# Where matmul operands lie in SBUF: weights of the seven-product tiles and of the down projection shifted by 128 bytes in a decoder layer on one core

## The chip, the core and the metric

One core of a Trainium2 chip runs one program: TensorE (matmuls; its weight loads are listed on their own as PEld), VectorE (DVE), ScalarE (ACT), GpSimd (POOL) and SyncE, which issues the weight transfers from HBM. The metric is device time in microseconds (us) of one execution.

## The reference

One decoder layer on x of 512 tokens by 1024 columns, all in float32:

```python
x = x + 0.5 * swiglu(rms_norm(x, g_ffn1), w_ffn1_gate, w_ffn1_up, w_ffn1_down)
h = rms_norm(x, g_mix); proj = h @ w_in
# sliding-window attention with sinks, causal depthwise convolution with layer norm,
# and cross-attention into 256 memory tokens, from column groups of proj
x = x + concatenate([y_attn, y_conv, y_mem]) @ w_out
x = x + 0.5 * swiglu(rms_norm(x, g_ffn2), w_ffn2_gate, w_ffn2_up, w_ffn2_down)

def swiglu(x, w_gate, w_up, w_down):
    return (silu(x @ w_gate) * (x @ w_up)) @ w_down
```

The feed-forward width is 2816: 22 tiles of 128 columns, called f = 0 to 21 below.

## The kernel before

Activations are held transposed, with 128 columns of the model on the partitions and 512 tokens along the free axis. To keep float32 accuracy, every large operand is split in two float32r parts, hi (a rounded copy) and lo (what the rounding lost), and each product is three matmuls: weights hi by moving hi, weights hi by moving lo, weights lo by moving hi. In a projection with 512 moving columns (helper `mm3`) these are L330, L331 and L332; in the products of a feed-forward tile (`product`) they are L434, L435 and L436, with 256 moving columns.

Each feed-forward stage (`ffn`, called as "fast1" and "fast2") runs f = 0 to 3 directly, with full gate and up projections (L330 to L332, moving tiles `xh`, `xl`). The other 18 tiles use a seven-product scheme of the Strassen kind over the 2 by 2 blocks gate/up by token halves: seven products of four blocks each, that is 84 matmuls of 256 columns (moving tiles `bh`, `bl`). The down projections (L330 to L332, moving tiles `hh`, `hl`, 512 columns) are done in rounds between the tiles, most of them after the fifth of the seven products. Between the two stages `mixing` does attention, convolution and memory attention by a list of steps in a fixed order (`ORDER`).

Weights pass through the class `Weights`. SyncE loads them into one of four `wraw` buffers (L138), ACT writes the hi part (L158, `whi`) and DVE the lo part (L159, `wlo`), each into a rotation of four buffers of 1024 columns. The second half of one weight tile of each seven-product tile goes to a buffer pair of its own, `vhi` and `vlo`, from the stage's pool (`extra`).

All these buffers lie in SBUF at fixed addresses. What counts below is the address within a partition, modulo 256 bytes. All `whi`, `wlo`, `vhi` and `vlo` start at 0; blocks of weights within them are 512 bytes apart, so that every weight block starts at 0. `xh`, `xl`, `yh`, `yl`, `hh`, `hl` start at 64. `bh` and `bl` start at 192 in the first feed-forward stage and at 64 in the second: the argument `shift` of `ffn`, 128 in the first call and 0 in the second, puts a pad of that many bytes ahead of the stage's pool, and a second pad after `bh` and `bl` brings both to one total. So the start of the moving tile less that of the weights is 192 in the first stage's products, 64 in the second's, and 64 in all down projections and other projections.

Two small things in `mixing` matter as well. `consts` (L745) fills a constant tile `avg` on POOL and a mask tile `maskb` of two rows of 512 columns on DVE, early in the stage. `ln_mean` (L1036) sums the two convolution tiles, takes their mean by a matmul with `avg` (L1042), and DVE subtracts it (L1044); squares on ACT (L1050), a sum on DVE (L1052) and small matmuls (L1057) follow.

Of the kernel before, what the change touches and what calls it, by code (L numbers as in the profile page):

```python
# [25 lines left out]
F32 = mybir.dt.float32  # L29
F32R = mybir.dt.float32r  # L30
BF16 = mybir.dt.bfloat16
# [5 lines left out]
P = 128  # L37
T = 512
# [43 lines left out]
class Weights:  # L82
# [5 lines left out]
    def __init__(self, nc, pool, dma_ahead, conv_ahead, bufs):  # L88
        self.nc, self.pool = nc, pool
        self.dma_ahead, self.conv_ahead, self.bufs = dma_ahead, conv_ahead, bufs  # L90
        self.loads, self.items = [], []
        self.raw, self.after, self.split, self.piece = {}, {}, {}, {}
        self.sums = {}
        self.extra = None
        self.by_hand = 2
        self.loaded = self.done = self.at = 0

    def add(self, ap):

        self.loads.append(ap)  # L100
        i = len(self.loads) - 1
        self.items.append((i, int(np.prod(ap.shape[1:])), "w", lambda: self.raw[i]))

    def add_pair(self, gate, up, mid):

        self.loads += [gate, up]
        i = len(self.loads) - 2
        self.after[i + 1] = lambda: self.make_sums(i)
        self.items.append((i, 1024, "w", lambda: self.raw[i]))
        self.items.append((i + 1, 1024, "w", lambda: self.sums[i][0]))  # L110
        self.items.append((i + 1, 1024, "w", lambda: self.sums[i][1]))
        for ap in mid:
            self.add(ap)
        self.items.append((i + 1, 512, "v", lambda: self.raw[i + 1][:, 512:]))

    def make_sums(self, i):
        nc = self.nc
# [23 lines left out]
    def split_to(self, n):  # L141
        nc = self.nc
        while self.done < min(n, len(self.items)):
            i = self.done
            need, cols, tag, src = self.items[i]
            self.load_to(need + 1)
            if need in self.after:
                self.after.pop(need)()
            pool = self.pool if tag == "w" else self.extra
            width = 1024 if tag == "w" else 512  # L150
            bufs = self.bufs[1:] if tag == "w" else (1, 1)
            hi = pool.tile([P, width], F32R, tag=tag + "hi", name=f"{tag}hi{i}", bufs=bufs[0])
            lo = pool.tile([P, width], F32R, tag=tag + "lo", name=f"{tag}lo{i}", bufs=bufs[1])
            if i < self.by_hand:
                self.piece[i] = (src(), hi, lo)
            else:
                raw = src()
                nc.scalar.copy(hi[:, :cols], raw[:, :cols])  # L158
                nc.vector.tensor_tensor(lo[:, :cols], raw[:, :cols], hi[:, :cols].bitcast(F32), op=ALU.subtract)  # L159
            self.split[i] = (hi, lo)  # L160
            self.done += 1
            if i >= self.by_hand:
                self.load_to(need + 1 + self.dma_ahead)
# [33 lines left out]
def layer(tc, ctx, a):  # L197
    nc = tc.nc
# [9 lines left out]
    def nm(s):  # L208
        uid[0] += 1
        return f"{s}_{uid[0]}"  # L210
# [14 lines left out]
        return tmp.tile([P, n], F32, tag=f"s{n}", name=nm("s"), bufs=6)  # L225


    W = Weights(nc, wpool, dma_ahead=3, conv_ahead=3, bufs=(4, 4, 4))

    def flat(w):  # L230
        return w.rearrange("p k m -> p (k m)")
# [1 line left out]
    def ffn_weights(n, memory):  # L233
        gu = a[f"wgu{n}"]

        def down(r, g):
            lo, hi = ROUNDS[r]
            m = per_load(r)
            return a[f"wd{n}"][g * m : (g + 1) * m, :, lo:hi].rearrange("d p k m -> p d (k m)")

        for f in range(NF):
            pre, mid, post = steps(f)
            for d in pre:
                W.add(down(*d))
            if f < N_DIRECT:
                W.add(flat(gu[f, 0]))
                W.add(flat(gu[f, 1]))
            else:
                W.add_pair(flat(gu[f, 0]), flat(gu[f, 1]), [down(*d) for d in mid])
            for d in post:  # L250
                W.add(down(*d))
            if memory and f == MEM_F:
                for t in range(2):
                    W.add(flat(a["wmk"][t]))
                for c in range(2):
                    W.add(flat(a["wmv"][:, 4 * c : 4 * c + 4]))
        r = len(ROUNDS) - 1
        for g in range(KT // per_load(r)):
            W.add(down(r, g))

    ffn_weights(1, True)
    for t in range(12):
# [116 lines left out]
                PE.transpose(ps[:, s], self.bc[:, s], ident)  # L379
            DVE.tensor_copy(rb, ps)  # L380

    def ffn(pool, norm, first, gain, hooks, next_gain, last, shift):
        if shift:
            pool.tile([P, shift // 4], F32, name=nm("shift"))
        h_hi = [None] * NF
        h_lo = [None] * NF
        W.extra = pool
# [19 lines left out]
        def blocks(k):  # L407
# [9 lines left out]
            bh[k] = pool.tile([P, 7, 256], F32R, tag="bh", name=nm("bh"), bufs=4)  # L417
            bl[k] = pool.tile([P, 7, 256], F32R, tag="bl", name=nm("bl"), bufs=4)
            if k == 0:
                pool.tile([P, (192 - shift) // 4], F32, name=nm("shift"))  # L420
            ACT.copy(bh[k][:, 4:7], raw[:, 0:3])
            DVE.tensor_tensor(made[:, B_T3 : B_Q1 + 1], raw[:, 1:3], raw[:, 3:4].to_broadcast([P, 2, 256]), op=ALU.subtract)
            DVE.scalar_tensor_tensor(made[:, B_Q2], made[:, B_T3], -1.0, b11, op0=ALU.mult, op1=ALU.subtract)
# [284 lines left out]
    hooks[MEM_F - 1] = [lambda: piece(2), lambda: piece(3)]  # L708
    hooks[MEM_F], hooks[MEM_F + 1] = [sums, p1], [p2]
    with tc.tile_pool(name="fast1", bufs=1) as pool:  # L710
        norm = ffn(pool, norm, STARTS, C_G1, hooks, C_GM, False, 128)

    with tc.tile_pool(name="mix", bufs=1) as mix:
        norm = mixing(tc, nc, a, mix, W, norm, locals())

    with tc.tile_pool(name="fast2", bufs=1) as pool:
        ffn(pool, norm, [[0, 1, 2, 3, 4, 5, 6], [7]], C_G2, {}, None, True, 0)


def mixing(tc, nc, a, mix, W, norm, e):  # L720
# [14 lines left out]
    vtok = mix.tile([P, NB, P], F32, name="vtok")  # L735
    for i in range(2):
        POOL.memset(pad[:, i, 0:30], 0.0)
    avg = mix.tile([P, P], F32, name="avg")
    maskb = mix.tile([P, 2, T], BF16, name="maskb")
    identb = mix.tile([P, P], BF16, name="identb")  # L740
    nsink = mix.tile([P, 8], F32, name="nsink")
    maskf = work()[:, :256]
    nc.scalar.dma_start(maskf, a["mask"])

    def consts():  # L745
        POOL.memset(avg, 1.0 / 256.0)
        DVE.tensor_copy(maskb[:, :, 0:256], maskf.unsqueeze(1).to_broadcast([P, 2, 256]))
        DVE.tensor_copy(maskb[:, :, 256:512], maskf.unsqueeze(1).to_broadcast([P, 2, 256]))
        DVE.memset(maskb[:, 0, 0:128], -1e30)
        DVE.tensor_copy(identb, ident)  # L750
        DVE.tensor_scalar(nsink, par[:, C_SINK : C_SINK + 8], -1.0, None, op0=ALU.mult)

# [85 lines left out]
    class Attend:  # L838
# [10 lines left out]
        def scores(self, j):  # L849

            self.banks[j] = banks = [sc_bank(), sc_bank()] if j == 0 else [mm_bank(), mm_bank()]
            if self.win:
                for h in range(2):
                    PE.matmul(banks[h], identb, maskb[:, j], start=True, stop=False, skip_group_check=True)
            for i in range(2):
                n = 2 * j + i
                c = self.cols(n)
                for h in range(2):
                    rows = slice(h * HD, (h + 1) * HD)
                    ks = slice((n - 1) * P + c.start, (n - 1) * P + c.stop) if self.win else slice(0, ML)  # L860
                    PE.matmul(  # L861
                        banks[h][:, i * ML + c.start : i * ML + c.stop], self.q[rows, n * P : (n + 1) * P],
                        self.kt[rows, ks], start=not self.win, stop=True, skip_group_check=True,
                    )
# [171 lines left out]

    def ln_mean():
        pump(TAPS)
        both = work()
        DVE.tensor_tensor(both, conv[:, 0], conv[:, 1], op=ALU.add)  # L1040
        mean = tp_bank()
        PE.matmul(mean, avg, both, start=True, stop=True)  # L1042
# [161 lines left out]
```

## Time and profile before

| | us |
|---|---|
| median of 3 runs | 891.36 |
| lowest and highest of them | 890.57, 891.64 |
| the profiled execution | 892.07 |
| its span | 890.1 |
| PE busy in the span | 878.1 |
| DVE busy | 713.4 |
| ACT busy | 440.0 |

The profiled execution is one run with the hardware profiler on; its span goes from the first instruction's start to the last one's end, and 2.0 us of its time lie outside. Matmuls are pipelined, and the length that the profile gives one (280 ns for 256 columns) overlaps the next. Its pace, the time from one matmul's start to the next one's, has to be worked out from the starts in the timeline. Those are given to 10 ns, so a pace is taken over many matmuls: last start less first, divided by the number of steps.

### The profile page before, as it was taken

How to read it: one execution, taken by the hardware profiler on the slowest of the kernel's cores; microseconds unless marked ns; L12 is line 12 of the kernel's file. 1: busy time of each engine (PE TensorE's matmuls, PEld its weight loads, DVE VectorE, ACT ScalarE, POOL GpSimd, SP SyncE). 2: the span in 40 equal slices, each digit the busy share in tenths (PEclk: the TensorE clock that was granted, in tenths of full speed). 3: DMA queues.
4: the chain of work that ended last, by engine and by line, in shares of the span. 5: the costliest groups of instructions: out<-in, count | busy, mean ns of one | idle time of the engine just before them, and what ended most of it. 6: DMA issues, size and time to landing. Idle time of an engine off the chain costs nothing.

```text
span 890.1 us, 13999 instructions
## 1 busy us (share of the span) xinstructions
PE 878.1 (99%) x5525; PEld 771.7 (87%) x5525; DVE 713.4 (80%) x1122; ACT 440.0 (49%) x733; POOL 45.6 (5%) x38
## 2 busy tenths in 40 slices
PE   7999999999999999999999999999999999999998
PEld 3889999999999999888666788889999999999997
DVE  6999978986796886769999766999887868667872
ACT  6354554544563444533928754444554444444540
POOL 6000000000020000300020011000000000000000
PEclk9999999999999999999999999999999999999999
DMA  5522333333333244231010232314333332332312
GB/s 194 166 95 81 109 120 107 113 102 118 111 128 123 92 119 142 72 100 60 9 52 13 83 117 74 103 64 142 95 96 119 96 118 83 109 116 73 119 48 95
DMA packets 34082, 88.45 MB, mean 99 GB/s; under 512 B 3168, under 2 KB 7008, under 8 KB 34016
## 3 DMA queue, kind: packets, MB, share of 16 engines
q1 hardware_dynamic: 32864, 85.99, 30.5%
q10 hardware_dynamic: 1152, 1.57, 0.5%
q8 instruction: 43, 0.70, 0.3%
q14 instruction: 23, 0.19, 0.1%
HBM read 85.45 MB, written 2.10 MB: 98 GB/s over the span
## 4 chain that ended last, share of the span: by engine, by line
PE 94%; DVE 3%; DMA 1%; issue 1%; ACT 0%; SPq 0%; DVEq 0%; ACTq 0%
PE mm L330 15%; PE mm L332 15%; PE mm L331 15%; PE mm L435 11%; PE mm L434 11%; PE mm L436 11%; PE sc L435 2%; PE sc L434 2%; PE sc L436 2%; PE sc L330 1%; PE sc L332 1%; PE sc L331 1%; PE tp L922 1%; PE sc L861 1%; DMA x<-in_xT 1%; DVE conv L786 1%
## 5 line engine op out<-in xcount | busy, mean ns | idle before, releaser
L435 PE MATMUL mm<-bl,whi 128*128 128x256 f32 x864 | 242.3, 280 | 0.0
L434 PE MATMUL mm<-bh,whi 128*128 128x256 f32 x864 | 242.2, 280 | 0.0
L436 PE MATMUL mm<-bh,wlo 128*128 128x256 f32 x864 | 241.9, 280 | 0.0
L158 ACT CAST whi<-wraw 128x1024 fp32r<-128x1024 f32 (+2 forms) x122 | 124.5, 1023 | 130.6 <-PE mm L331 51.0
L159 DVE TENSOR_TENSOR wlo<-wraw,whi 128x1024 fp32r<-128x1024 f32 (+2 forms) x122 | 144.7, 1187 | 35.6 <-ACT whi L158 35.3
L436 PEld LDWEIGHTS mm<-bh,wlo 128*128 128x128 f32 x864 | 163.5, 189 | 0.0
L434 PEld LDWEIGHTS mm<-bh,whi 128*128 128x128 f32 x864 | 162.3, 188 | 1.2 <-ACT kept L449 0.2
L435 PEld LDWEIGHTS mm<-bl,whi 128*128 128x128 f32 x864 | 162.3, 188 | 1.1
L330 PE MATMUL mm<-hh,whi 128*128 128x512 f32 (+1 forms) x356 | 138.5, 392 | 0.0
L332 PE MATMUL mm<-hh,wlo 128*128 128x512 f32 (+1 forms) x356 | 138.2, 390 | 0.0
L331 PE MATMUL mm<-hl,whi 128*128 128x512 f32 (+1 forms) x356 | 137.4, 387 | 0.0
L159 DVE TENSOR_TENSOR wlo<-s,whi 128x1024 fp32r<-128x1024 f32 x72 | 88.3, 1228 | 34.4 <-ACT whi L158 33.7
L158 ACT CAST whi<-s 128x1024 fp32r<-128x1024 f32 x72 | 75.4, 1048 | 56.3 <-PE mm L435 40.2
L332 PEld LDWEIGHTS mm<-hh,wlo 128*128 128x128 f32 x356 | 66.8, 188 | 15.3
L332 PE MATMUL mm<-xh,wlo 128*128 128x512 f32 x192 | 76.9, 400 | 2.3 <-DVE wlo L171 2.3
L330 PE MATMUL mm<-xh,whi 128*128 128x512 f32 x192 | 77.7, 406 | 1.5 <-ACT whi L170 1.5
L331 PEld LDWEIGHTS mm<-hl,whi 128*128 128x128 f32 x356 | 66.8, 188 | 12.5
L331 PE MATMUL mm<-xl,whi 128*128 128x512 f32 x192 | 76.4, 398 | 1.1 <-DVE xl L342 1.0
L330 PEld LDWEIGHTS mm<-hh,whi 128*128 128x128 f32 x356 | 66.9, 188 | 11.7
L491 DVE SCALAR_TENSOR_TENSOR x<-mm,x 128x512 f32<-128x512 f32 x88 | 59.3, 682 | 9.1 <-PE mm L332 9.0
L158 ACT CAST vhi<-wraw 128x512 fp32r<-128x512 f32 x36 | 22.3, 620 | 55.0 <-PE sc L435 40.1
L455 ACT ACTIVATE t<-t 128x512 f32<-128x512 f32 x36 | 22.8, 632 | 52.8 <-DVE t L454 52.7
(246 smaller groups left out, 1397.9 us busy)
## 6 DMA issues: line engine op xcount, KB each, us to landing
wraw<-in_wgu SPq DMA_DIRECT2D x86, 512.0 KB, 3.5
wraw<-in_wd SPq DMA_DIRECT2D x44, 512.0 KB, 3.6
wraw<-in_win SPq DMA_DIRECT2D x12, 512.0 KB, 3.4
out<-t SPq DMA_DIRECT2D x7, 256.0 KB, 2.0
x<-in_xT SPq DMA_DIRECT2D x3, 512.0 KB, 6.0
wraw<-in_wout_a SPq DMA_DIRECT2D x6, 256.0 KB, 2.6
t<-in_memT ACTq DMA_DIRECT2D x4, 256.0 KB, 3.4
wraw<-in_wmk SPq DMA_DIRECT2D x2, 512.0 KB, 4.1
```

Source lines behind the costliest of these rows:

```text
L158: nc.scalar.copy(hi[:, :cols], raw[:, :cols])
L159: nc.vector.tensor_tensor(lo[:, :cols], raw[:, :cols], hi[:, :cols].bitcast(F32), op=ALU.subtract)
L330: PE.matmul(ps, wh[:, w], hi(k), start=first and i == 0, stop=False)
L331: PE.matmul(ps, wh[:, w], lo(k), start=False, stop=False)
L332: PE.matmul(ps, wl[:, w], hi(k), start=False, stop=last and i == len(ks) - 1)
L434: PE.matmul(ps, wh[:, c], bh[k][:, block], start=one, stop=False, skip_group_check=not first)
L435: PE.matmul(ps, wh[:, c], bl[k][:, block], start=False, stop=False, skip_group_check=not first)
L436: PE.matmul(ps, wl[:, c], bh[k][:, block], start=False, stop=end, skip_group_check=not first)
L455: ACT.activation(g, g, AF.Silu)
L491: DVE.scalar_tensor_tensor(o, ps, 0.5, xd, op0=ALU.mult, op1=ALU.add)
L786: DVE.scalar_tensor_tensor(conv[:, i], pad[:, i, j : j + T], w(i, j), conv[:, i], op0=ALU.mult, op1=ALU.add)
L861: PE.matmul(banks[h][:, i * ML + c.start : i * ML + c.stop], self.q[rows, n * P : (n + 1) * P], self.kt[rows, ks], start=not self.win, sto ...
```

## The change

The weights' hi and lo buffers become 1056 columns wide, that is 128 bytes wider, and each set of weights says at which offset in its buffer it wants to lie (`off`, 0 or 128 bytes). The four slots become four tags used in turn. A `wlo` buffer starts 128 bytes off a `whi` buffer, and the offset within it is the complement, so that hi and lo start at the same place modulo 256. Weights of the seven products and of the down projections ask for 128, all others for 0. The pads in `ffn` become one pad of 64 bytes, the argument `shift` goes, and `bh` and `bl` start at 64 in both stages; `vhi` and `vlo` start at 128.

Moving start less weight start is then 192 in all seven-product tiles (before: 192 in the first stage, 64 in the second), 192 in all down projections (before: 64), and 64 in the other projections, as before. All moving tiles of these start at 64.

To make room, `maskb` shrinks from two rows of 512 to three of 256, of which the mask's matmul reads two next to each other, and one DVE cast takes the place of two. `avg` loses its own tile and is filled in a work buffer at the head of `ln_mean`.

```diff
-    def add(self, ap):
+    def add(self, ap, off=0):
...
-        self.items.append((i, 1024, "w", lambda: self.raw[i]))
-        self.items.append((i + 1, 1024, "w", lambda: self.sums[i][0]))
-        self.items.append((i + 1, 1024, "w", lambda: self.sums[i][1]))
+        self.items.append((i, 1024, 128, lambda: self.raw[i]))
+        self.items.append((i + 1, 1024, 128, lambda: self.sums[i][0]))
+        self.items.append((i + 1, 1024, 128, lambda: self.sums[i][1]))
         for ap in mid:
-            self.add(ap)
-        self.items.append((i + 1, 512, "v", lambda: self.raw[i + 1][:, 512:]))
+            self.add(ap, 128)
+        self.items.append((i + 1, 512, None, lambda: self.raw[i + 1][:, 512:]))
...
-            pool = self.pool if tag == "w" else self.extra
-            width = 1024 if tag == "w" else 512
-            bufs = self.bufs[1:] if tag == "w" else (1, 1)
-            hi = pool.tile([P, width], F32R, tag=tag + "hi", name=f"{tag}hi{i}", bufs=bufs[0])
-            lo = pool.tile([P, width], F32R, tag=tag + "lo", name=f"{tag}lo{i}", bufs=bufs[1])
+            if off is None:
+                hi, lo = (self.extra.tile([P, cols], F32R, tag=t, name=f"{t}{i}", bufs=1) for t in ("vhi", "vlo"))
+            else:
+                j = self.turn % self.bufs[1]
+                self.turn += 1
+                hi, lo = (
+                    self.pool.tile([P, 1024 + 32], F32R, tag=f"{t}{j}", name=f"{t}{i}", bufs=1)[:, c : c + 1024]
+                    for t, c in (("whi", off // 4), ("wlo", 32 - off // 4))
+                )
...
-                W.add(down(*d))
+                W.add(down(*d), 128)
...
-    def ffn(pool, norm, first, gain, hooks, next_gain, last, shift):
-        if shift:
-            pool.tile([P, shift // 4], F32, name=nm("shift"))
+    def ffn(pool, norm, first, gain, hooks, next_gain, last):
...
-                pool.tile([P, (192 - shift) // 4], F32, name=nm("shift"))
+                pool.tile([P, 16], F32, name=nm("shift"))
...
-    avg = mix.tile([P, P], F32, name="avg")
-    maskb = mix.tile([P, 2, T], BF16, name="maskb")
+    maskb = mix.tile([P, 3, 2 * P], BF16, name="maskb")
...
     def consts():
-        POOL.memset(avg, 1.0 / 256.0)
-        DVE.tensor_copy(maskb[:, :, 0:256], maskf.unsqueeze(1).to_broadcast([P, 2, 256]))
-        DVE.tensor_copy(maskb[:, :, 256:512], maskf.unsqueeze(1).to_broadcast([P, 2, 256]))
-        DVE.memset(maskb[:, 0, 0:128], -1e30)
+        DVE.tensor_copy(maskb, maskf.unsqueeze(1).to_broadcast([P, 3, 2 * P]))
+        DVE.memset(maskb[:, 0, 0:P], -1e30)
...
     def ln_mean():
         pump(TAPS)
-        both = work()
+        both, avg = work(), work()[:, :P]
+        POOL.memset(avg, 1.0 / 256.0)
```

The order of instructions on PE, DVE, ACT and SyncE stays what it was through both feed-forward stages. It moves at one place, around the layer norm of the convolution at the end of `mixing`. On DVE there stood (`wlo` tiles are the lo parts of `w_out`, `conv` the convolution's result, `tp` a PSUM bank):

```order
L953 TENSOR_TENSOR yl_3989<-tp_5206,yh_3981 128x512
L159 TENSOR_TENSOR wlo_5224<-wraw_4955,whi_5223 128x1024
L1044 TENSOR_TENSOR conv<-conv,tp_5250 128x512 x2
L159 TENSOR_TENSOR wlo_5296<-wraw_5012,whi_5295 128x512
L1052 TENSOR_TENSOR t_5256<-t_5254,t_5256 128x512
```

and now stand, with the changed kernel's own line numbers:

```order
L955 TENSOR_TENSOR yl_3988<-tp_5202,yh_3980 128x512
L166 TENSOR_TENSOR wlo_5220<-wraw_4951,whi_5219 128x1024
L166 TENSOR_TENSOR wlo_5294<-wraw_5008,whi_5293 128x512
L1047 TENSOR_TENSOR conv<-conv,tp_5248 128x512 x2
L1055 TENSOR_TENSOR t_5254<-t_5252,t_5254 128x512
```

The lo part of 512 columns now stands ahead of the subtraction of the mean, where it stood behind. On PE the small matmuls that follow (L1057, now L1060) stood three matmuls earlier. On POOL there stood, around the old place of the fill (`mtot` and `sqsum` are sums of squares, `pad` the convolution's input):

```order
L592 TENSOR_TENSOR mtot<-mtot,t_2798 128x512
L592 TENSOR_TENSOR mtot<-mtot,t_2807 128x512
L737 MEMSET pad 128x30 x2
L746 MEMSET avg 128x128
L359 TENSOR_TENSOR sqsum_3802<-sqsum_3802,t_3822 128x512
```

and around the new one now stand (L835 are the rotary products, L366 the sums of the next norm):

```order
L835 TENSOR_TENSOR t_4678<-t_4678,sinb 128x512
L835 TENSOR_TENSOR t_4780<-t_4780,sinb 128x512
L835 TENSOR_TENSOR t_5031<-t_5031,sinb 128x512
L1042 MEMSET t_5245 128x128
L366 TENSOR_TENSOR sqsum_5441<-sqsum_5441,t_5454 128x512
```

The fill of the tile for the mean has moved from ahead of one norm's sums to behind the last rotary product.

More of the change, by code (lines that the diff above doesn't have):

```diff
@@ L95, in __init__ @@
         self.by_hand = 2
-        self.loaded = self.done = self.at = 0
-    def add(self, ap):
+        self.loaded = self.done = self.at = self.turn = 0
+    def add(self, ap, off=0):
         self.loads.append(ap)
         i = len(self.loads) - 1
-        self.items.append((i, int(np.prod(ap.shape[1:])), "w", lambda: self.raw[i]))
+        self.items.append((i, int(np.prod(ap.shape[1:])), off, lambda: self.raw[i]))
     def add_pair(self, gate, up, mid):
@@ L144, in split_to @@
             i = self.done
-            need, cols, tag, src = self.items[i]
+            need, cols, off, src = self.items[i]
             self.load_to(need + 1)
@@ L225, in small @@
         return tmp.tile([P, n], F32, tag=f"s{n}", name=nm("s"), bufs=6)
-    W = Weights(nc, wpool, dma_ahead=3, conv_ahead=3, bufs=(4, 4, 4))
+    W = Weights(nc, wpool, dma_ahead=3, conv_ahead=3, bufs=(4, 4))
     def flat(w):
@@ L250, in ffn_weights @@
             for d in post:
-                W.add(down(*d))
+                W.add(down(*d), 128)
             if memory and f == MEM_F:
@@ L258, in ffn_weights @@
         for g in range(KT // per_load(r)):
-            W.add(down(r, g))
+            W.add(down(r, g), 128)
     ffn_weights(1, True)
@@ L710, in layer @@
     with tc.tile_pool(name="fast1", bufs=1) as pool:
-        norm = ffn(pool, norm, STARTS, C_G1, hooks, C_GM, False, 128)
+        norm = ffn(pool, norm, STARTS, C_G1, hooks, C_GM, False)
     with tc.tile_pool(name="mix", bufs=1) as mix:
@@ L716, in layer @@
     with tc.tile_pool(name="fast2", bufs=1) as pool:
-        ffn(pool, norm, [[0, 1, 2, 3, 4, 5, 6], [7]], C_G2, {}, None, True, 0)
+        ffn(pool, norm, [[0, 1, 2, 3, 4, 5, 6], [7]], C_G2, {}, None, True)
 def mixing(tc, nc, a, mix, W, norm, e):
@@ L853, in scores @@
                 for h in range(2):
-                    PE.matmul(banks[h], identb, maskb[:, j], start=True, stop=False, skip_group_check=True)
+                    PE.matmul(banks[h], identb, maskb[:, j : j + 2].rearrange("p a b -> p (a b)"), start=True, stop=False, skip_group_check=True)
             for i in range(2):
```

## The prediction

> **What bounds the kernel now.** I read the page first: who is busy, and of whom the chain that ended last is made.
>
> ```profile
> PE 878.1 (99%) x5525; PEld 771.7 (87%) x5525; DVE 713.4 (80%) x1122; ACT 440.0 (49%) x733; POOL 45.6 (5%) x38
> PE 94%; DVE 3%; DMA 1%; issue 1%; ACT 0%; SPq 0%; DVEq 0%; ACTq 0%
> ```
>
> PE is busy for 99% of the span and is 94% of the chain. Next, what PE waits for by the view of waits (line and tile, releaser, total us, times, longest):
>
> ```profile
> PE mm L332 <- DVE wlo L171: 2.3, 3, 0.9
> ...
> PE mm L330 <- ACT p L886: 0.3, 1, 0.3
> ```
>
> All nine of its rows add up to 8.7 us. So a faster or slower DVE, ACT or transfer buys next to nothing; the time is the number of matmuls times their pace. The groups that the change touches, by shape (count | busy us, mean ns):
>
> ```profile
> L435 PE MATMUL mm<-bl,whi 128*128 128x256 f32 x864 | 242.3, 280 | 0.0
> L330 PE MATMUL mm<-hh,whi 128*128 128x512 f32 x348 | 136.3, 394 | 0.0
> L435 PE MATMUL sc<-bl,vhi 128*128 128x256 f32 x144 | 40.4, 280 | 0.0
> ```
>
> L434 and L436 have the same counts as L435, so there are 3 x (864 + 144) = 3024 product matmuls, half in each stage, and 3 x 348 = 1044 matmuls of the down projection with 512 columns (the 24 half-width ones at the end are left aside). The mean lengths are modelled and overlap; the pace comes from starts in PE's timeline (start us, length us, line, names).
>
> In the first stage, moving tiles lie 192 bytes from the weights. The first and the last of 144 products that follow each other:
>
> ```profile
> 76.45 0.28 PE L434 MATMUL mm<-bh,whi 128*128 128x256 f32 x1
> ...
> 93.29 0.28 PE L436 MATMUL mm<-bh,wlo 128*128 128x256 f32 x1
> ```
>
> 143 steps in 16.84 us: **117.8 ns**. In the second stage they lie 64 bytes away, and again 144 follow each other:
>
> ```profile
> 603.95 0.28 PE L434 MATMUL mm<-bh,whi 128*128 128x256 f32 x1
> ...
> 620.80 0.28 PE L436 MATMUL mm<-bh,wlo 128*128 128x256 f32 x1
> ```
>
> 143 steps in 16.85 us: **117.8 ns** as well (117.83 against 117.76). The kernel before thus holds the very comparison that the change is about, for the products, and it shows no difference. The down projection, 64 bytes away, 114 matmuls that follow each other:
>
> ```profile
> 346.74 0.40 PE L330 MATMUL mm<-hh,whi 128*128 128x512 f32 x1
> ...
> 372.62 0.39 PE L332 MATMUL mm<-hh,wlo 128*128 128x512 f32 x1
> ```
>
> 113 steps in 25.88 us: **229.0 ns**. Together the touched matmuls are 3024 x 0.1178 + 1044 x 0.229 = 595 us, two thirds of the span, so that one per cent of pace would be 6 us.
>
> One stretch doesn't fit. After four transposes (L662) the products of one tile of the first stage ran faster, until the next down projection (L330):
>
> ```profile
> 309.97 0.60 PE L662 MATMUL tp<-ident,t 128*128 128x128 f32 x4
> 310.32 0.37 PE L434 MATMUL mm<-bh,whi 128*128 128x256 f32 x1
> 310.53 0.28 PE L435 MATMUL mm<-bl,whi 128*128 128x256 f32 x1
> ...
> 317.11 0.28 PE L436 MATMUL mm<-bh,wlo 128*128 128x256 f32 x1
> 317.22 0.40 PE L330 MATMUL mm<-hh,whi 128*128 128x512 f32 x1
> ```
>
> From 310.53 to 317.22 there are 59 steps: **113.4 ns**, 4.4 below the others. The granted clock cannot explain it; the view by stretches has it at 1.00 there, its most:
>
> ```profile
> 310.50:317.00 6.50, 6.50 (x60) 6.50 (x58) 6.19 (x9) 4.13 (x7) 0.00 (x0) 1.00 0.55 164
> ```
>
> (PE, PEld, DVE, ACT, POOL, then PEclk.) So the same instructions have two steady paces on PE, and which one holds depends on how the stream was entered. This is the only opening for a gain.
>
> **The change part by part.** *Products of the first stage* keep 192: 0. The fast stretch stays if the distance decides; if it went, it would cost 59 x 4.4 ns = 0.26 us.
>
> *Products of the second stage* go from 64 to 192: 1512 x (117.76 - 117.83) ns = -0.1 us.
>
> *Down projections* go from 64 to 192. The trace has no 512-column matmul at 192, so I bound it from both sides. Below: the fast stretch saves 4.4 ns per 256 columns; per matmul that is 1044 x 4.4 = -4.6 us, per column 1044 x 8.8 = -9.2 us. Above: the slowest steps of a down projection that wait for nothing are those right behind the products of the first stage, where moving tiles change from 192 to 64:
>
> ```profile
> 128.61 0.40 PE L330 MATMUL mm<-hh,whi 128*128 128x512 f32 x1
> ...
> 129.08 0.40 PE L332 MATMUL mm<-hh,wlo 128*128 128x512 f32 x1
> ```
>
> Two steps in 0.47 us, 235 ns, 6 over the steady pace: 1044 x 6 = +6.3 us. I take 0, since the nearest rows, the two long stretches of products, put 192 and 64 equal; both ends stay in the range.
>
> Here a rule of the Trainium skill speaks against the change. The page "TensorE: Matmul & The Clock Gate", section "Step-by-step: what each phase is for", says that PE has two independent SBUF read ports, and that loading the next weights takes no read bandwidth from the running matmul. By it the distance cannot matter and this term is 0; by the rows it is 0 with ends at -9.2 and +6.3. The two equal paces agree with the rule; the stretch at 113.4 ns is not explained by it.
>
> *Conversion of weights* (L158, L159) has the same instructions, sizes and order in both stages; its buffers merely start elsewhere: 0. A few per cent on ACT or DVE would hide behind PE, as its 8.7 us of waits show.
>
> *Mask* (L747, L748): two casts become one of three quarters of their elements.
>
> ```profile
> L747 DVE CAST maskb<-t x1: 415/415/415, 380.1 to 380.1; 128x512 bf16<-128x512 f32 x1
> L748 DVE CAST maskb<-t x1: 415/415/415, 380.5 to 380.5; 128x512 bf16<-128x512 f32 x1
> 380.00:430.00 50.00, 50.00 (x241) 39.79 (x240) 41.68 (x99) 21.25 (x40) 0.00 (x0) 1.00 0.20 68
> ```
>
> 0.83 us of DVE become about 0.62. PE is busy in all 50 us that follow, so it is worth 0; without that cover it would be -0.2 us.
>
> *Layer norm of the convolution* (L1042 to L1057). A `wlo` of 0.68 us now stands ahead of the subtraction L1044:
>
> ```profile
> 503.07 1.21 DVE L159 TENSOR_TENSOR wlo<-wraw,whi 128x1024 fp32r<-128x1024 f32 x1
> 504.51 1.28 DVE L1044 TENSOR_TENSOR conv<-conv,tp 128x512 f32<-128x512 f32 x2 [0.23 <-PE tp L1042]
> 505.72 0.68 DVE L159 TENSOR_TENSOR wlo<-wraw,whi 128x512 fp32r<-128x512 f32 x1
> 506.62 0.69 DVE L1052 TENSOR_TENSOR t<-t,t 128x512 f32<-128x512 f32 x1 [0.22 <-ACT t L1050]
> ```
>
> DVE had 0.23 us to spare there, so L1044 and what hangs on it (ACT's squares, L1052, PE's L1057) come about 0.45 us later. PE fills that with projections of `yh`, of which one more now stands ahead of L1057; queued behind L1057 on PE are transposes and further projections, which would lose at most that 0.45 us. I take 0, with +0.5 as the upper end; the lower is 0, because nothing there gets earlier. The fill of `avg` moves to a POOL that is idle:
>
> ```profile
> L746 POOL MEMSET avg<- x1: 205/205/205, 347.9 to 347.9; 128x128 f32 x1
> 471.09 1.28 POOL L833 TENSOR_TENSOR t<-t,sinb 128x512 f32<-128x512 f32 x1 [9.90 <-DVE t L832]
> 527.30 1.30 POOL L359 TENSOR_TENSOR sqsum<-sqsum,t 128x512 f32<-128x512 f32 x1 [54.93 <-ACT t L355]
> ```
>
> Between 472.4 and 527.3 POOL has nothing else, and the matmul that reads the fill starts at 503.4: 0, and at most its own 0.2 us.
>
> *Sum*: -0.1 us. On the profiled execution's footing that is 892.07 - 0.1 = 892.0 (span 890.1 and 2.0 around it); that execution lies 0.7 above the median of the runs shown, so for a median I say 891.36 - 0.1 = **891.3 us**. A measurement of this kernel can tell about 0.2%, 1.8 us, from no change.
>
> **The rivals.** *The fast pace spreads.* If a down projection at 192 no longer throws the stream out of the fast pace, or falls into it by itself, the gain is large. For it: both paces exist for one instruction stream; the fast one was seen only at 192, and ended with the first matmul at 64. At 64 a restart after transposes did not bring it:
>
> ```profile
> 33.43 0.60 PE L379 MATMUL tp<-ident,t 128*128 128x128 f32 x4
> ...
> 34.10 0.40 PE L331 MATMUL mm<-xl,whi 128*128 128x512 f32 x1
> ...
> 59.75 0.39 PE L332 MATMUL mm<-xh,wlo 128*128 128x512 f32 x1
> ```
>
> 112 steps in 25.65 us, 229.0 ns. Against it: at 192, too, nearly all products run at 117.8, among them those after another restart (L638):
>
> ```profile
> 299.19 0.95 PE L638 MATMUL tp<-pair,t 128*128 128x2 f32 x8
> ...
> 300.20 0.28 PE L435 MATMUL mm<-bl,whi 128*128 128x256 f32 x1
> ...
> 309.85 0.28 PE L436 MATMUL mm<-bh,wlo 128*128 128x256 f32 x1
> ```
>
> 82 steps in 9.65 us, 117.7 ns. The price has three sizes: the down projections alone, -4.6 to -9.2 us, 882 to 887; one whole stage, about half of everything, 880; all products and down projections, (3024 - 59) x 4.4 ns = 13.0 and 9.2, -22 us, **869**.
>
> *The fast pace only lasts longer.* It begins after L662, as before, and holds through the down projections to the end of the first stage. There are left then:
>
> ```profile
> L434 PE MATMUL mm<-bh,whi x52: 279/281/282, 320.0 to 346.4; 128*128 128x256 f32 x52
> L434 PEld LDWEIGHTS sc<-bh,vhi x12: 187/188/188, 318.4 to 344.9; 128*128 128x128 f32 x12
> L330 PE MATMUL mm<-hh,whi x48: 394/394/398, 317.2 to 372.2; 128*128 128x512 f32 x48
> ```
>
> 3 x 64 x 4.4 ns + 3 x 48 x 8.8 ns = 2.1 us: 889.2. The stages between and behind run at 64 again.
>
> *The down projection gets slower at 192.* One mechanism, L330 to L332 of `hh` and `hl`: what only the entry steps pay now, 235 ns, every step pays. +6.3 us: **897.6**. It decides from 1.8 us / 1044 = 1.7 ns more per matmul. Against it: the products at 192 pay nothing over those at 64.
>
> *The change doesn't do what it says*, in that not the distance but the moving tile's own place decides. All moving tiles then lie at 64, where the fast pace was never seen, and the stretch at 113.4 goes: +0.3 us, no change.
>
> **How the numbers follow.** No measurable change (the forecast, with the last rival in it): 0.45. The fast pace spreads: 0.32, of which a third each for its three sizes. It only lasts longer: 0.13. Slower down projection: 0.10. Faster by over 0.2% is then 0.32 + 0.13 = 0.45, within 0.2% 0.45, slower 0.10. The forecast's own range is 890 to 893. For 8 in 10 the range goes down to 879, which leaves out the largest spread (0.1), and up to 893, which leaves out the slower rival (0.1).
>
> **What would show it.** Starts in the timeline, not the modelled lengths. Right: products of the second stage at 117.8, down projections at 229.0, the stretch after L662 at 113.4. Spread: down projections near 220 to 225, products at 113.4 in long stretches. Slower: down projections near 235. The layer norm: L1044's successor about 0.45 us later, and a PE wait of at most that before the small matmuls. The forecast is wrong if any long stretch of 512-column matmuls at 192 keeps another pace than 229.

## The result

| | us |
|---|---|
| before, median of 6 runs | 891.63 |
| after, median of 6 runs | 884.29 |
| lowest and highest of after | 883.23, 884.99 |
| ratio, with its 95% interval | 0.9917, 0.9904 to 0.993 |
| span of the profiled execution, before and after | 890.1, 883.2 |

The changed kernel is 0.8% faster, 7.3 us. The time lies inside the predicted range, but not where the forecast put it: no change was taken as likeliest. The range reached so far down for the sake of the rivals alone. The page of after, its first part (busy time by engine) and the engines of its chain:

```profile
PE 869.9 (98%) x5522; PEld 760.4 (86%) x5525; DVE 713.1 (81%) x1121; ACT 438.2 (50%) x733; POOL 45.9 (5%) x38
PE 93%; DVE 4%; DMA 1%; issue 1%; ACT 0%; SPq 0%; DVEq 0%
```

PE is still the bound; its chain is as closed as before, so the gain must be pace. PE's timeline of after (start us, length us, line, names), with the changed kernel's lines: products are L439 to L441, 512-column matmuls L337 to L339. The first and the last of three stretches without a gap: 144 products of the first stage, 114 down projections, 228 products of the second stage.

```profile
75.80 0.28 PE L439 MATMUL mm<-bh,whi 128*128 128x256 f32 x1
...
92.01 0.28 PE L441 MATMUL mm<-bh,wlo 128*128 128x256 f32 x1
...
343.31 0.39 PE L337 MATMUL mm<-hh,whi 128*128 128x512 f32 x1
...
369.67 0.39 PE L339 MATMUL mm<-hh,wlo 128*128 128x512 f32 x1
...
626.02 0.28 PE L439 MATMUL mm<-bh,whi 128*128 128x256 f32 x1
...
651.75 0.28 PE L441 MATMUL mm<-bh,wlo 128*128 128x256 f32 x1
```

143 steps in 16.21 us and 227 in 25.73: **113.4 ns** per product in both stages, the fast pace that was seen in one stretch before (117.8 elsewhere). 113 steps in 26.36 us: **233.3 ns** per down projection, where it was 229.0. So two things came at once, with opposite signs.

The fast pace is a state that the stream of matmuls is in or not. Of 2962 product steps, taken in groups of twelve and without those over 135 ns, which hold a wait or another delay, 2462 are in groups with a mean below 116 ns (called fast below); before it was 58 of 2966. Here it is lost and found again in the first stage of after:

```profile
124.81 0.28 PE L441 MATMUL mm<-bh,wlo 128*128 128x256 f32 x1
124.93 0.32 PE L439 MATMUL mm<-bh,whi 128*128 128x256 f32 x1
125.09 0.28 PE L440 MATMUL mm<-bl,whi 128*128 128x256 f32 x1
...
134.79 0.28 PE L439 MATMUL mm<-bh,whi 128*128 128x256 f32 x1
...
141.74 0.28 PE L441 MATMUL mm<-bh,wlo 128*128 128x256 f32 x1
...
171.91 0.28 PE L441 MATMUL mm<-bh,wlo 128*128 128x256 f32 x1
172.50 0.39 PE L439 MATMUL mm<-bh,whi 128*128 128x256 f32 x1 [0.30 <-ACT kept L454]
172.72 0.28 PE L440 MATMUL mm<-bl,whi 128*128 128x256 f32 x1
```

One step of 160 ns at 124.93, and from there every step is slow, through several rounds of down projections: 59 steps from 134.79 to 141.74 are 117.8 each. A wait of 0.30 us for ACT at 172.50, and behind it the steps are 113 again; a wait of 0.36 us at 170.51, two microseconds earlier, had left them slow. The clock has no part in it. The view by stretches (us; busy time of PE, PEld, DVE, ACT, POOL; granted clock; DMA share; GB/s), in the slow stretch and in a fast one:

```profile
134.80:141.70 6.90, 6.90 (x60) 6.90 (x59) 6.44 (x9) 4.24 (x7) 0.00 (x0) 1.00 0.35 88
626.10:651.70 25.60, 25.60 (x228) 25.60 (x227) 21.89 (x29) 16.07 (x26) 0.00 (x0) 1.00 0.34 104
```

There is one mark by which the state can be told. The view of one line (least, median and longest length in ns) shows for PEld, the weight loads, in after's slow stretch and then in its fast one:

```profile
L440 PEld LDWEIGHTS mm<-bl,whi x20: 188/192/192, 134.8 to 141.5; 128*128 128x128 f32 x20
L440 PEld LDWEIGHTS mm<-bl,whi x68: 187/188/188, 626.0 to 651.5; 128*128 128x128 f32 x68
```

At the slow pace one of the three loads of a block takes 192 ns instead of 188. With that, the kernel before reads differently. Its two stages, both at 117.8 ns, distance 192 first and 64 second:

```profile
L436 PEld LDWEIGHTS mm<-bh,wlo x42: 192/192/193, 76.9 to 92.8; 128*128 128x128 f32 x42
L436 PEld LDWEIGHTS mm<-bh,wlo x42: 187/187/188, 604.1 to 620.0; 128*128 128x128 f32 x42
```

Equal paces, but the first stage has the mark and the second hasn't. In the first the stream keeps the slow one of two paces; in the second, as the experiments show, 117.8 is simply what distance 64 gives. The mark holds without exception in the traces kept here of this kernel, the changed one and the experiments, s2 aside: of the products at distance 192, taken in whole groups of twelve steps away from the ends of a round, 546 slow groups have one of the three loads at 192 ns (by its median) and 1086 fast ones have none; nor has any of 218 groups at distance 64, all slow.

The account of the 6.9 us of span, from the starts of both traces: 2462 - 58 more fast steps at 4.4 ns, -10.6; longer delays within the products, +1.0; the down projections, +3.6; the start-up, -1.0. That is -7.0. The down projections cost less than 1044 x 4.3 ns = 4.5 us, because the kernel before, too, paid slow first steps in its rounds of twelve between products (229.9 to 230.4 ns per step there, now 232.6 to 233.0). The start-up is not put down to the change: the first down projection starts 0.97 us earlier, but in the profiled executions here of all kernels that start lies between 58.4 and 60.3, and in two of the changed kernel alone at 59.0 and 58.4.

### The profile page after: what moved, and what is told of

Same layout as the page of the kernel before. It is cut to its first block, busy times and chain, and to the rows that moved or that the text cites. A ratio compares the mean times of both kernels' runs of the same rounds, so it can differ in the third digit from the quotient of the medians.

```text
span 883.2 us, 13993 instructions
## 1 busy us (share of the span) xinstructions
PE 869.9 (98%) x5522; PEld 760.4 (86%) x5525; DVE 713.1 (81%) x1121; ACT 438.2 (50%) x733; POOL 45.9 (5%) x38
## 4 chain that ended last, share of the span: by engine, by line
PE 93%; DVE 4%; DMA 1%; issue 1%; ACT 0%; SPq 0%; DVEq 0%
PE mm L337 15%; PE mm L339 15%; PE mm L338 15%; PE mm L439 11%; PE mm L441 11%; PE mm L440 11%; PE sc L439 2%; PE sc L441 2%; PE sc L440 2%; PE sc L337 1%; PE sc L339 1%; PE sc L338 1%; PE tp L924 1%; PE sc L863 1%; DVE conv L788 1%
## 5 line engine op out<-in xcount | busy, mean ns | idle before, releaser
L439 PE MATMUL mm<-bh,whi 128*128 128x256 f32 x864 | 239.8, 278 | 0.7 <-ACT kept L450 0.4
L441 PE MATMUL mm<-bh,wlo 128*128 128x256 f32 x864 | 239.2, 277 | 0.0
L440 PE MATMUL mm<-bl,whi 128*128 128x256 f32 x864 | 239.2, 277 | 0.0
L439 PEld LDWEIGHTS mm<-bh,whi 128*128 128x128 f32 x864 | 162.3, 188 | 2.2 <-ACT kept L450 0.6
L440 PEld LDWEIGHTS mm<-bl,whi 128*128 128x128 f32 x864 | 162.7, 188 | 1.2
L441 PEld LDWEIGHTS mm<-bh,wlo 128*128 128x128 f32 x864 | 162.2, 188 | 0.0
L339 PE MATMUL mm<-hh,wlo 128*128 128x512 f32 (+1 forms) x356 | 139.4, 393 | 0.0
L338 PE MATMUL mm<-hl,whi 128*128 128x512 f32 (+1 forms) x356 | 139.4, 393 | 0.0
L337 PE MATMUL mm<-hh,whi 128*128 128x512 f32 (+1 forms) x356 | 138.6, 392 | 0.0
L339 PEld LDWEIGHTS mm<-hh,wlo 128*128 128x128 f32 x356 | 66.9, 188 | 15.4
L339 PE MATMUL mm<-xh,wlo 128*128 128x512 f32 x192 | 76.4, 398 | 2.8 <-DVE wlo L178 2.8
L337 PEld LDWEIGHTS mm<-hh,whi 128*128 128x128 f32 x356 | 66.9, 188 | 13.5
L337 PE MATMUL mm<-xh,whi 128*128 128x512 f32 x192 | 76.6, 401 | 0.6 <-ACT whi L177 0.6
```

Source lines behind the costliest of these rows:

```text
L337: PE.matmul(ps, wh[:, w], hi(k), start=first and i == 0, stop=False)
L338: PE.matmul(ps, wh[:, w], lo(k), start=False, stop=False)
L339: PE.matmul(ps, wl[:, w], hi(k), start=False, stop=last and i == len(ks) - 1)
L439: PE.matmul(ps, wh[:, c], bh[k][:, block], start=one, stop=False, skip_group_check=not first)
L440: PE.matmul(ps, wh[:, c], bl[k][:, block], start=False, stop=False, skip_group_check=not first)
L441: PE.matmul(ps, wl[:, c], bh[k][:, block], start=False, stop=end, skip_group_check=not first)
```

## The experiments

Each kernel is the changed one with the edit shown. Times are medians beside runs of the kernel before on the same chip.

**Each half alone.** e1_down64 puts the down projections back to distance 64, e2_prod64 the products.

```diff
# e1_down64
-                W.add(down(*d), 128)
+                W.add(down(*d))
...
# e2_prod64
-        self.items.append((i, 1024, 128, lambda: self.raw[i]))
+        self.items.append((i, 1024, 0, lambda: self.raw[i]))
...
-                pool.tile([P, 16], F32, name=nm("shift"))
+                pool.tile([P, 48], F32, name=nm("shift"))
```

> The changed kernel with one part undone: the weights of the down projections back at offset 0, so that their moving tiles lie 64 bytes away again; the products stay at 192 with weights at 128 and moving tiles at 64. Theory A (the pace of the products is a state of PE's stream; a down projection at 64 leaves the stream in the slow state, one at 192 leaves it in whichever it was): products fall back to 117.7 ns behind every down projection, down projections go back from 233.3 to 229.0 ns, so about 884.3 + 2370 x 4.3 ns - 1044 x 4.3 ns = 890 us. Rival B (what helps the products is their own new place, weights at 128 and moving tiles at 64, and the down projection has no part in it): products stay at 113.4, down projections at 229.0, about 884.3 - 4.5 = 880 us.

> The other part undone: down projections at 192 as in the changed kernel, products at 64 in both stages (weights at 0, moving tiles at 64). Theory A: the fast state exists for products at 192 alone, so all products run at 117.8 and the down projections at 233.3: about 884.3 + 2370 x 4.4 ns = 894.7 us, slower than the kernel before. Rival C (a down projection at 192 brings the fast state to whatever follows, wherever the products lie): products stay at 113.4, about 884 us.

e1_down64: **882.05 us**, 0.989 [0.9872, 0.9909]. e2_prod64: **895.03 us**, 1.0039 [1.0025, 1.0053]. PE's timeline of e1: 114 down projections that follow each other, and the second stage's 228 products:

```profile
341.35 0.39 PE L337 MATMUL mm<-hh,whi 128*128 128x512 f32 x1
...
367.21 0.39 PE L339 MATMUL mm<-hh,wlo 128*128 128x512 f32 x1
...
623.33 0.28 PE L439 MATMUL mm<-bh,whi 128*128 128x256 f32 x1
...
649.07 0.28 PE L441 MATMUL mm<-bh,wlo 128*128 128x256 f32 x1
```

113 steps in 25.86 us, 228.8 ns per down projection, and 227 in 25.74, 113.4 per product: the gain without the loss. Of its 2960 product steps 2784 are fast. That the products need down projections at 192 to stay fast was wrong. In e2, 144 products that follow each other:

```profile
605.86 0.28 PE L439 MATMUL mm<-bh,whi 128*128 128x256 f32 x1
...
622.71 0.28 PE L441 MATMUL mm<-bh,wlo 128*128 128x256 f32 x1
```

117.8 ns, none of 2968 steps is fast, and down projections at 233.3. Down projections at 192 do not bring the fast pace by themselves; they only cost. Halves and whole fit together: e2 lies 3.6 us over the kernel before of its round (891.4), which is what the steps of after's down projections add up to.

**All distances in one kernel.** s1_downscan gives each load of down weights another distance, with products at 192; s2_prodscan gives each seven-product tile another, with down projections at 192. The buffers become 1088 columns wide, and to make room two kinds of tile lose a buffer each.

```diff
+SCAN = {1: [192, 0, 32, 64, 96, 128, 160, 224], 2: [64, 224, 160, 128, 96, 32, 0, 192]}
-                W.add(down(*d), 128)
+                W.add(down(*d), off())     # s1: (64 - next of SCAN) mod 256
...
```

> A scan in one kernel: products at 192 throughout, each load of down projection weights at another distance from its moving tiles (192, 0, 32, 64, 96, 128, 160, 224 bytes in turn in the first stage, another order in the second). Buffers are 128 bytes wider, and there is one buffer fewer of kept and of pt to make room. Read are paces, not the time. Theory A: the down projection's own pace depends on its distance (229.0 at 64, 233.3 at 192), and the products behind it are slow after 64, fast or as they were after 192; other distances are open. Rival B: the products behind keep one pace, 113.4, whatever the distance of the down projection.

> A scan in one kernel: down projections at 192 throughout, the products of each tile at another distance (192, 0, 32, 64, 96, 128, 160, 224 bytes in turn in the first stage, another order in the second), with the wider buffers of the other scan. Theory A: 113.4 ns at 192 and 117.8 at 64, other distances open. Rival C: one pace at all distances. If distance counts only modulo 128, 0 and 128 agree with each other, 32 with 160, 96 with 224, and 64 with 192; the two paces at 64 and 192 speak against that.

One run of each: 888.23 and 896.11 us. In s2's timeline, 60 products at 192 and, a few tiles on, 60 at 64:

```profile
184.01 0.28 PE L440 MATMUL mm<-bh,whi 128*128 128x256 f32 x1
...
190.70 0.28 PE L442 MATMUL mm<-bh,wlo 128*128 128x256 f32 x1
...
230.16 0.28 PE L440 MATMUL mm<-bh,whi 128*128 128x256 f32 x1
...
237.11 0.28 PE L442 MATMUL mm<-bh,wlo 128*128 128x256 f32 x1
```

113.4 and 117.8 ns. Worked out in that way for every distance from the starts of both traces (steps with a wait left out):

| distance | products, s2: ns per step (steps) | down projections, s1: ns per step in rounds of 12 | products behind them, s1 |
|---|---|---|---|
| 0 | 119.6 (411) | 229.1 to 229.2 | slow, 6 of 6 (4 fast ahead) |
| 32 | 116.7 (329) | 233.1 to 233.6 | fast, 4 of 4 (3 fast ahead) |
| 64 | 117.8 (412) | 228.6 fast, 230.1 slow | as ahead of them, 8 of 8 |
| 96 | 119.9 (327) | 233.6 to 233.7 | fast, 5 of 6 (4 fast ahead) |
| 128 | 119.1 (329) | 231.9 to 232.6 | fast stays (2); slow stays or turns (2 each) |
| 160 | 117.7 (329) | 233.8 to 234.7 | slow, 5 of 5 (2 fast ahead) |
| 192 | 113.4, once 117.8 (412) | 232.6 fast, 232.9 slow | as ahead of them, 6 of 6 |
| 224 | 118.3 (408) | 233.0 to 234.0 | the other state, 5 of 5 |

For 256 columns 192 is the one of these eight distances with the fast pace, and for 512 columns 64 and 0 are the two good ones, so the change has the right number for the products and the wrong one for the down projections. A round of twelve hides that distance 0 settles to the shortest step of all. In s1, behind the first six of 18 in a row at distance 0:

```profile
345.09 0.39 PE L340 MATMUL mm<-hh,whi 128*128 128x512 f32 x1
...
347.58 0.40 PE L342 MATMUL mm<-hh,wlo 128*128 128x512 f32 x1
```

11 steps in 2.49 us, 226 to 227 ns, where 64 settles at 228.9. The first six cost 231.3 each, and products behind are slow, so between products it is no gain; in long rows of other projections no run tries it.

The last column is what no expectation had: the products' state is handed through the down projections in between, or changed by them, by their distance. In s1, products at one and the same distance of 192, ahead of two rounds of down projections at distance 0 and behind them:

```profile
676.22 0.28 PE L442 MATMUL mm<-bh,whi 128*128 128x256 f32 x1
...
682.92 0.28 PE L444 MATMUL mm<-bh,wlo 128*128 128x256 f32 x1
683.03 0.40 PE L340 MATMUL mm<-hh,whi 128*128 128x512 f32 x1
...
691.35 0.28 PE L442 MATMUL mm<-bh,whi 128*128 128x256 f32 x1
...
698.30 0.28 PE L444 MATMUL mm<-bh,wlo 128*128 128x256 f32 x1
```

59 steps in 6.70 us, 113.6 ns, and 59 in 6.95, 117.8.

**Distance, place or entry.** The kernel before has 192 in its first stage and stays slow there; e1 has 192 and is fast. Four kernels with the products at 192 tell three theories apart:

| | products: moving, weights | down projections: moving, weights | steps at a changeover |
|---|---|---|---|
| e3_prodmove | 192, 0 | 64, 0 (distance 64) | moving tile |
| e4_down64_shift | 192, 0 | 192, 128 (distance 64) | weights |
| e5_bothmove | 192, 0 | 64, 128 (distance 192) | both |
| e6_shift | 192, 0 | 192, 0 (distance 192) | neither |

```diff
# e3, e5: the stage's pool 128 bytes further, products' weights at 0 (e3: down weights too)
+        pool.tile([P, 32], F32, name=nm("shift"))
-        self.items.append((i, 1024, 128, lambda: self.raw[i]))
+        self.items.append((i, 1024, 0, lambda: self.raw[i]))
...
# e4, e6: all activations 128 further, products' weights at 0 (e6: down weights too), others at 128
-    tmp.tile([P, 32], F32, name="shift")
-    def add(self, ap, off=0):
+    def add(self, ap, off=128):
...
```

> The changed kernel with another pair of places at the same distances as e1_down64: products 192 from their weights (moving tile at 192, weights at 0, where e1 had moving 64, weights 128), down projections 64 (moving 64, weights 0, as in e1). Entering products, the moving tile's place changes (64 to 192) and the weights' stays; in e1 it was the other way round. Theory D (only the distance decides): 882, as e1_down64. Theory P (the place of the products' own tiles decides): products at 117.8, 891.5. Theory S (the step of places at the changeover decides, and a steady run of products or of down projections at 64 keeps the state that it was entered with): first stage slow as in the kernel before, which had these places there; second stage the same, 891.5.

> e1_down64 with every address of weights and moving tiles 128 further (mod 256): products moving 192, weights 0; down projections moving 192, weights 128, so that the weights step at a changeover and the moving tile stays, as in e1_down64. Theory D: 882. Theory P (the products' own places, those of the kernel before's first stage): 891.5. Theory S (the step): 882, fast products (113.4) behind down projections at 229.

> Products with moving tile at 192 and weights at 0, down projections with moving tile at 64 and weights at 128: all of them 192 apart, as in the changed kernel, but at each changeover both places step by 128. Theory D (only the distance decides): 884, as the changed kernel. Theory P (place of the products' own tiles): 895, as e2_prod64, with products at 117.8 and down projections at 233.3. Theory S (the step at the changeover) gives no size: 884 if both steps cancel, 895 if the moving tile's step decides; the first gap behind a down projection and the pace tell which.

> The changed kernel with weights and moving tiles of the products and down projections 128 further (mod 256): moving 192, weights 0 for both; nothing steps at a changeover, distance 192 throughout. Theory D and theory S: 884, as the changed kernel, products at 113.4, down projections at 233.3. Theory P: 895, products at 117.8.

| | us | ratio to before | interval | fast steps |
|---|---|---|---|---|
| e3_prodmove | 891.86 | 1.0003 | 0.9993 to 1.0013 | 68 of 2967 |
| e4_down64_shift | 879.9 | 0.9873 | 0.9856 to 0.9889 | 2162 of 2965 |
| e5_bothmove | 892.03 | 0.9997 | 0.9973 to 1.002 | 258 of 2968 |
| e6_shift | 886.57 | 0.9938 | 0.9918 to 0.9958 | 1837 of 2967 |

e3 and e4 have the same products at the same addresses, and down projections at the same distance of 64; the place of the down projections differs, by 128 bytes, and in e4 that of the other activations and projections with it. The same 228 products of the second stage, first and last, in e3's timeline:

```profile
629.59 0.28 PE L440 MATMUL mm<-bh,whi 128*128 128x256 f32 x1
...
656.32 0.28 PE L442 MATMUL mm<-bh,wlo 128*128 128x256 f32 x1
```

and in e4's, where L438 to L440 are the same lines:

```profile
624.30 0.28 PE L438 MATMUL mm<-bh,whi 128*128 128x256 f32 x1
...
650.04 0.28 PE L440 MATMUL mm<-bh,wlo 128*128 128x256 f32 x1
```

227 steps in 26.73 us, 117.8 ns, against 227 in 25.74, 113.4. The mark goes with it: the loads of the third line in that stretch, by line, in e3

```profile
L442 PEld LDWEIGHTS mm<-bh,wlo x66: 192/192/192, 630.1 to 655.9; 128*128 128x128 f32 x66
```

and in e4

```profile
L440 PEld LDWEIGHTS mm<-bh,wlo x68: 187/188/188, 624.4 to 649.9; 128*128 128x128 f32 x68
```

So theory D falls with e3 (882 expected, 891.86 measured) and theory P with e4 (891.5 expected, 879.9 measured): neither the distance nor the products' own places decide alone; how the products lie to the down projections between them matters too. Theory S is what is left, with a limit: between the four kernels the crossing decides whether a fast pace outlasts a round of down projections, not in which state a stage begins. In e3, behind the transposes at 310, 60 products ran fast, then six down projections, then 24 products:

```profile
310.65 0.28 PE L441 MATMUL mm<-bl,whi 128*128 128x256 f32 x1
...
317.23 0.28 PE L442 MATMUL mm<-bh,wlo 128*128 128x256 f32 x1
...
318.73 0.28 PE L440 MATMUL sc<-bh,vhi 128*128 128x256 f32 x1
...
321.44 0.28 PE L442 MATMUL mm<-bh,wlo 128*128 128x256 f32 x1
```

58 steps in 6.58 us, 113.4 ns, and 23 in 2.71, 117.8: behind a round at which the moving tile steps the fast pace was gone. At the same place of e4, where the weights step, the 24 products behind kept 113.8. But e4, too, hands on a slow pace: in its profiled execution all products of the first stage up to 172 us ran so, at the addresses that were fast from there on, and 228 of them are

```profile
101.08 0.28 PE L438 MATMUL mm<-bh,whi 128*128 128x256 f32 x1
...
127.81 0.28 PE L440 MATMUL mm<-bh,wlo 128*128 128x256 f32 x1
```

227 steps in 26.73 us, 117.8 ns, with the mark. Two steps of 0.22 to 0.23 us at 172.64 ended that; e4_again below has 2941 fast steps with the same kernel. So one kernel can differ by its state from execution to execution. e5 says the same: the state is kept, whichever it is. Its profiled execution is slow nearly throughout, but at these same addresses 144 products, reached fast from the transposes at 310 on, stayed fast:

```profile
326.03 0.28 PE L440 MATMUL mm<-bh,whi 128*128 128x256 f32 x1
...
342.24 0.28 PE L442 MATMUL mm<-bh,wlo 128*128 128x256 f32 x1
```

143 steps in 16.21 us, 113.4 ns; its ten runs lie between 885.2 and 893.9, wider than those of e3 (891.0 to 892.3). e6 lies 2.6 above the 884 that D and S gave it: in its profiled execution the first stage ran slow for nearly all of its first 300 us, the second stage fast. There, as in the changed kernel, nothing steps, and a slow pace is handed on as well as a fast one.

At one place of the first stage the state turns in all nine traces with products at 192 throughout in which it is not the moving tile alone that steps (after, e1, e4, e5, e6 and the four of the next table). One down projection stands alone there, and the other eleven of its round come 24 products later. In after:

```profile
246.85 0.39 PE L337 MATMUL mm<-hh,whi 128*128 128x512 f32 x1
247.08 0.28 PE L439 MATMUL mm<-bh,whi 128*128 128x256 f32 x1
...
249.79 0.28 PE L441 MATMUL mm<-bh,wlo 128*128 128x256 f32 x1
```

The products ahead of the single one run at 113.5 ns, the 24 behind it at 117.8 (23 steps in 2.71 us) and those behind the eleven at 113.6; in e5 and e6 it went from slow to fast and back. The exception at 96 in the table of distances is this round of eleven. All other rounds have an even number of matmuls, so that an odd number turns the state would fit; with this one place it is not shown.

**The two best side by side, and the cost away from the down projections.** e7_proj192 moves all other 512-column weights to distance 192 as well.

```diff
-    def add(self, ap, off=0):
+    def add(self, ap, off=128):
```

> The changed kernel again, unchanged, to stand beside the others of this round: 884.3 by every theory.

> e1_down64 again (products 192, down projections 64), beside the changed kernel on one chip. If the down projections' 4.3 ns per matmul are real and stay apart from the products' gain, it is 1044 x 4.3 ns = 4.5 us below the changed kernel where both run their products fast, less what it loses in the slow state and at its slower entries (some 40 changeovers x 12 ns = 0.5 us): 2 to 4 us below. If the first round's 2.2 us were chance, the two are within 1 us.

> e4_down64_shift again. Theory D and theory S: it is e1_down64 in another place, so the same time within 2 us. If the place matters by itself after all, it stays apart from e1 with the intervals not overlapping.

> The changed kernel with the weights of all other 512-column products (projections of x and y and their like, 864 matmuls) at 128 too, so 192 from their moving tiles instead of 64. If 233.3 ns is the pace of any 512-column product at 192, 864 x 4.3 ns = 3.7 us more than the changed kernel, 888; the part that waits anyway (start-up transfers, the interleaved middle stage) may hide up to half of it: 886 to 888. If the 4.3 ns come from the down projections standing between products, nothing: 884.3.

| | us | ratio to before | interval | fast steps |
|---|---|---|---|---|
| a2_changed | 883.72 | 0.9912 | 0.9899 to 0.9926 | 2858 of 2963 |
| e1_again | 880.55 | 0.988 | 0.9866 to 0.9893 | 2929 of 2962 |
| e4_again | 881.53 | 0.9896 | 0.9881 to 0.9911 | 2941 of 2964 |
| e7_proj192 | 886.7 | 0.9946 | 0.9932 to 0.9959 | 2941 of 2964 |

e1 is 3.2 us below the changed kernel, inside the 2 to 4 expected, and the intervals do not overlap: **products at 192 and down projections at 64 beat both kernels**. The intervals of e1 and e4 overlap, so no difference between their places is shown. e7 is 3.0 above the changed kernel, inside 886 to 888. In its timeline, 48 projections of `xh` and `xl`, ahead of any wait:

```profile
369.35 0.39 PE L337 MATMUL mm<-xh,whi 128*128 128x512 f32 x1
...
380.32 0.40 PE L339 MATMUL mm<-xh,wlo 128*128 128x512 f32 x1
```

47 steps in 10.97 us, 233.4 ns: the price of 192 belongs to 512 columns, not to what the matmuls stand between.

## Where the prediction was right and where wrong, point by point

*What bounds the kernel*: right. PE remained the bound and the whole difference is pace.

*Products of the second stage*, -0.1 us: wrong, and with it the first stage's 0. Together their faster steps are -10.6 us. The step that failed is the reading that the kernel before "holds the very comparison that the change is about, for the products, and it shows no difference". It compared two paces, but at 192 there are two, and the first stage showed the slow one; why that one equals the pace at 64 to 0.1 ns, no run shows. The prediction had the one fast stretch in hand, at 192 and at a granted clock of 1.00, and called it the only opening; it should have asked which of the two paces the stage was in, and the lengths of the loads, 192 against 187 ns, would have said that the two stages were slow for different reasons.

*Down projections*, 0 with ends at -9.2 and +6.3: wrong, since that 0 came from the same two rows. They cost +3.6 us. The rival was right in its sign and had over half of its size: in steady rows every step pays (233.3), a little less than the entry steps from which 235 was taken, but the kernel before paid at its entries already. The lower end went wrong for a clear reason: 256 and 512 columns have their best distances in different places, so the saving of the one says nothing of the other.

*The rivals* were treated as alternatives, and the time alone would have named the wrong one: 884.3 lies in the 882 to 887 that the prediction gave to faster down projections, which in fact got slower. Two of them came together: the fast pace spread over most products of both stages (at 13.0 us for all of them a fair size, of which 10.6 came), and the down projection got slower. The condition for the spread, that a down projection at 192 no longer throws the stream out of the fast pace, is met: 192 hands the state on in 6 of 6 rounds. But it is not needed, since e1 is fast with down projections at 64. What threw the kernel before out is, as far as e3 and e4 tell, its moving tile's step from 192 to 64 and back.

*That not the distance but the moving tile's own place decides*: no. At the same places 192 and 0, products ran slow in e3 and fast in most of e4.

*Mask, layer norm, fill of `avg`*: 0, right as far as it can be seen. From the last of the 114 down projections of the first stage to the first of the second stage it was 587.47 - 372.62 = 214.85 us, and now 584.58 - 369.67 = 214.91. None of these edits was tried alone.

The Trainium skill, page "TensorE: Matmul & The Clock Gate", section "Step-by-step: what each phase is for", gives PE two independent read ports, by which loading the next weights takes no read bandwidth from the running matmul. The runs do not bear out what the prediction drew from that, that the distance cannot matter: with PE busy without a gap and the clock at 1.00, one stream of 256-column matmuls runs at 113.4 or at 116.7 to 119.9 ns by addresses alone, and the slow pace at 192 shows in a weight load.

**What stays open**: why the two streams get in each other's way. The profile has no row for reads of SBUF, so a phase between the two readers, which a state that is kept, turned or lost at changeovers suggests, is an argument and not shown. Nor is it settled why a short delay sometimes ends the fast pace (the step of 160 ns at 124.93), sometimes brings it (the wait of 0.30 us at 172.50) and sometimes does neither (0.36 us at 170.51), or what sets the state in which a stage begins.

## What to carry to other kernels

When the same instruction shows two steady paces in one trace, find out which state each long stretch is in before taking equal paces as "no effect"; the lengths of the weight loads can tell it when the matmuls' modelled lengths don't. Choose SBUF places per shape (here the start of the moving tile less that of the weights, mod 256: 192 for 256 columns, and 64 for 512 columns between them), measured in one kernel that scans them. Keep the moving tiles at one place across a changeover, so that only the weights step (e1 and e4 here).

## What the runs showed of the hardware

- Addresses of weights and moving tile alone are worth up to 6% of PE's pace for 256 columns, 113.4 to 119.9 ns, and up to 3% for 512, 228.6 to 234.7 (table above).
- The pace has a memory. One step of 160 ns put the products of after onto the slow pace for 47 us, through rounds of down projections. With the moving tiles at one place (s1), rounds of down projections at 64 and 192 handed the state on, those at 224 reversed it, and behind those at 0 and 160 it was slow. A single down projection between products turned it in nine of nine traces.
- Down projections at 64 have a slower pace too. In e1, behind products that had turned slow at 830 us, the last 102 ran so:

```profile
849.71 0.40 PE L337 MATMUL mm<-hh,whi 128*128 128x512 f32 x1
...
873.27 0.40 PE L339 MATMUL mm<-hh,wlo 128*128 128x512 f32 x1
```

  101 steps in 23.56 us are 233.3 ns each, as at 192, where the same kernel's others took 228.8.
